# Fifteen blocks of an input projection moved ahead of attention and computed by fifteen products

## The chip, the core and the metric

The kernel runs on one core of one Trainium2 chip. The metric is the device time of one execution in microseconds (us), the median of several runs; lower is better. A core has one matrix engine (TensorE, PE in the profile, with its weight loads as PEld), three engines for elementwise work (VectorE is DVE, ScalarE is ACT, GpSimd is POOL) and queues that issue DMAs (SyncE is SP; here ACT issues some too). Each engine works through its own instructions in order, so an instruction that waits holds up all that stand behind it on that engine.

## What is computed

One layer of a streaming encoder for 1024 prompt frames and 32 sample frames, all in 32-bit floats. Both kinds of frames are treated together as T = 1056 columns. Cut to what matters here:

```
h = rmsnorm(x, g_mix) * (1 + sc1) + sh1
u = h @ w_in
qa, ka, va, qm, km, vm, om, ip, fp, ga, gm = split(u)
ya = band_attention(qa, ka, va)                      # 8 heads x 64
q_m, k_m = silu(causal_conv(concat(qm, km)))         # width 4
hm = mlstm(q_m, k_m, vm, ip, fp)                     # 4 heads x 128, a recurrence over blocks
ym = head_rmsnorm(hm) * sigmoid(om)
merged = sigmoid(ga) * (ya @ w_br_att) + sigmoid(gm) * (ym @ w_br_mlstm)
x = x + gt1 * (merged @ w_out)
x = x + gt2 * ((silu(h2 @ w_gate) * (h2 @ w_up)) @ w_down)
```

The gates `sc1`, `gt1` and so on are six vectors from `silu(c) @ w_ada + b_ada`.

## The kernel before

**Layout and blocks.** Features stand on the 128 partitions, the 1056 columns are cut in three thirds of 352 (`TILES`). A block of a projection is 128 output features. `unit` (L418) computes one third of one block: eight slices of 128 input features, and three matmuls for each slice (`PASSES`: high part times high, low times high, high times low, which is how the 32-bit product is kept accurate). So a plain block is 3 x 8 x 3 = 72 matmuls of 352 columns. The weights of a block are loaded (L404) and split in a high part by ACT (L394) and a low part by DVE or POOL (L395); `Weights` does that a fixed number of blocks ahead.

**Side work.** `unit` calls `side.tick()` after every second slice, so four times a third and twelve times a block. At a tick, generators started with `side.start(gen, steps, ticks, delay)` advance by `steps / ticks` steps. So the instructions of attention, of the recurrence and of the modulation are written between the matmuls of plain blocks, at a spacing that the table `segs` sets. All four compute engines keep exactly that order.

**The input projection.** The 40 blocks of q, k, v, convolution inputs, output gates `om` and merge gates `ga`, `gm` (and `vm` in two wide blocks, `vm_block`) are all computed plainly, in the order of `segs`: 3 blocks; then attention over pairs of heads 0, 1 and 2, beside 5, 5 and 7 blocks (three for the next q, k, v, the rest gates); attention 3 beside `vm_block(0)` and four convolution blocks; `mlstm(0)`, the recurrence of heads 0 and 1, beside `vm_block(1)` and four convolution blocks; and `mlstm(1)` followed by `branch_operands` beside twelve blocks (four `om`, eight gates). The modulation `ada_rest` (128 multiply-adds on DVE, L1139 and L1141, each two reading one DMA of 256 KB) runs beside all of this at 160 steps per 495 ticks.

**The recurrence.** `mlstm` goes through nine blocks of 128 columns. In the round for block i, a first step issues the scores and transposes of block i on PE (L1026, L1028) and the transposes of the result of block i-3 (L1096); a second step issues on DVE the scaling of result i-2 (L1090), the weighting of block i (L1044), and then the state update (L1070), the sum (L1073) and the denominators (L1077 to L1079) of block i-1, on PE the three products of block i-1 (L1056, L1059, L1061), on ACT its squares (L1082), and on POOL the two small operations that make the norm (L1084, L1085), which the scaling of the next round reads.

**The branch operands.** After `mlstm(1)`, for each of four blocks: sigmoid on ACT (L1183), a product on DVE (L1184), a split (L394 on ACT, L395 on DVE); then four splits of the attention result. The merge matmuls that follow read all of them.

**Fifteen products.** The feed-forward network already uses a scheme in which three blocks are computed together as a 3 x 2 by 2 x 3 product of sub-blocks with fifteen block products of 12 matmuls each (`Fifteen`, `fifteen_products`, `times` at L1726), 180 matmuls where plain blocks need 216. It needs sums of sub-blocks of the activations (`early_forms`, `late_forms`: sums at L1563 on DVE and POOL, high parts on ACT, low parts at L1576 on DVE) and sums of weight sub-blocks (L1361 on POOL).

## Time and profile before

| what | value |
| --- | --- |
| median of 3 runs | 1644.96 us (1642.6 to 1649.06) |
| the profiled execution | 1642.54 us |
| its span in the profile | 1640.6 us |
| PE busy | 1589.7 us (97%) |
| DVE busy | 1121.0 us (68%) |
| ACT busy | 780.8 us (48%) |
| POOL busy | 535.7 us (33%) |

The rows shown below come from five views: the page, the table of stretches (columns: from and to, length, then busy time of PE, PEld, DVE, ACT and POOL with their instruction counts, the granted clock of PE, the DMA share and GB/s), the groups by line (busy time and mean ns, then the idle time before them), the timeline (start, duration, engine, line, operation, tiles) and the chain that ended last. Since PE is busy nearly all the time, the question for any change is where PE starts to wait.

### The profile page before, as it was taken

To read this page: it belongs to the slowest core of one execution; us is meant where nothing else is said; L and a number is where in the kernel's file an instruction comes from. 1 tells how busy PE (TensorE), PEld (TensorE's weight loads), DVE (VectorE), ACT (ScalarE), POOL (GpSimd) and SP (SyncE) were. 2 spreads that over 40 slices of the span, in tenths; PEclk is the share of its full clock that TensorE was granted. 3 is DMA by queue.
4 is the path that set the end of the run, shared out by engine and by line. 5 is a ranking of instruction groups with operands and counts; after the bars stand their busy time and mean duration, and the time that the engine had idled before them with its cause. 6 is when DMAs were issued, how large, how long until landed. Compare 5 with 4: busy or idle time off the path is not lost.

```text
span 1640.6 us, 27517 instructions
## 1 busy us (share of the span) xinstructions
PE 1589.7 (97%) x10324; PEld 1566.7 (95%) x10324; DVE 1121.0 (68%) x2100; ACT 780.8 (48%) x1732; POOL 535.7 (33%) x540
## 2 busy tenths in 40 slices
PE   7989999999999999999999998999999999999997
PEld 6989999999999999999999988999999999999997
DVE  6756564546776744546655689889888986698754
ACT  3456454543455544444434645454545444444443
POOL 1234333333332311000012155566565742233101
PEclk9999999999999999999999999999999999999999
DMA  9732323232222332584453211313222236427453
GB/s 344 251 98 75 111 75 106 67 126 75 84 83 78 67 94 66 131 273 152 128 151 109 91 53 39 105 53 104 79 82 88 78 102 216 141 65 238 134 157 123
DMA packets 210326, 192.45 MB, mean 117 GB/s; under 512 B 10570, under 2 KB 180530, under 8 KB 209170
## 3 DMA queue, kind: packets, MB, share of 16 engines
q1 hardware_dynamic: 205970, 188.60, 36.8%
q10 hardware_dynamic: 4224, 2.10, 0.4%
q8 instruction: 81, 1.33, 0.4%
q14 instruction: 51, 0.42, 0.1%
HBM read 152.19 MB, written 41.63 MB: 118 GB/s over the span
## 4 chain that ended last, share of the span: by engine, by line
PE 79%; DVE 8%; ACT 3%; issue 2%; DMA 1%; POOL 1%; DVEq 0%; POOLq 0%; ACTq 0%
PE mm L428 35%; PE psb L1726 24%; PE psb L2082 5%; PE mm L825 3%; PE psb L1967 3%; PE psV L725 2%; PE psS L667 1%; DVE wsp L395 1%; PE psT L694 1%; DVE s L395 1%; DVE s L1576 1%; DVE s L1989 1%; DVE sl L1563 1%; DVE st L681 1%; PE psV L1059 1%
## 5 line engine op out<-in xcount | busy, mean ns | idle before, releaser
L428 PE MATMUL mm<-s,wsp 128*128 128x352 f32 x4104 | 690.4, 324 | 5.8 <-DVE t L1657 1.9
L428 PEld LDWEIGHTS mm<-s,wsp 128*128 128x128 f32 x4104 | 656.8, 188 | 9.0 <-DVE stg L518 2.3
L1726 PE MATMUL psb<-s,wsp 128*128 128x352 f32 x2544 | 422.0, 323 | 11.4 <-DVE s L1989 5.5
L1726 PEld LDWEIGHTS psb<-s,wsp 128*128 128x128 f32 x2544 | 410.9, 189 | 14.4 <-issue 6.1
L395 DVE TENSOR_TENSOR wsp<-wraw,wsp 128x512 fp32r<-128x512 f32 (+1 forms) x284 | 246.0, 884 | 136.0 <-ACT wsp L394 134.2
L394 ACT ACTIVATE wsp<-wraw 128x512 fp32r<-128x512 f32 x340 | 201.5, 617 | 147.6 <-PE psb L1726 84.5
L687 POOL TENSOR_SCALAR st<-st,mx 128x640 f32<-128x640 f32 (+5 forms) x72 | 57.0, 791 | 193.7 <-DVE mx L686 179.5
L1141 DVE SCALAR_TENSOR_TENSOR t<-wa,cmix,t 128x512 f32<-128x512 f32 x112 | 88.8, 797 | 8.9 <-DMA wa<-in_w_ada_dram 8.5
L395 POOL TENSOR_TENSOR wsp<-wraw,wsp 128x512 fp32r<-128x512 f32 x56 | 73.8, 1339 | 52.4 <-ACT wsp L394 52.0
L2082 PE MATMUL psb<-s,wsp 128*128 128x352 f32 x528 | 86.7, 324 | 0.0
L2082 PEld LDWEIGHTS psb<-s,wsp 128*128 128x128 f32 x528 | 84.7, 188 | 0.0
L681 DVE CUSTOM_DVE_ANT_0 st<-psS,bias 128x640 f32<-128x640 f32 (+5 forms) x72 | 44.5, 618 | 57.8 <-PE psS L667 44.9
L1726 PE MATMUL psb<-x,wsp 128*128 128x352 f32 x432 | 80.2, 325 | 2.3 <-DVE x L1576 2.3
L682 ACT ACTIVATE st<-st,mx 128x640 f32<-128x640 f32 (+5 forms) x72 | 47.9, 666 | 67.5 <-DVE mx L681 67.5
L1676 POOL TENSOR_TENSOR t<-t,sl 128x352 f32<-128x352 f32 x18 | 17.4, 969 | 185.3 <-ACT sl L1674 185.3
L1726 PEld LDWEIGHTS psb<-x,wsp 128*128 128x128 f32 x432 | 71.5, 189 | 2.8 <-DVE x L1576 2.8
L701 ACT ACTIVATE pT<-psT 128x640 fp32r<-128x640 f32 (+3 forms) x80 | 38.7, 494 | 72.1 <-PE psT L694 55.1
L1764 DVE TENSOR_TENSOR t<-t,psb 128x352 f32<-128x352 f32 x120 | 60.4, 512 | 5.2 <-PE psb L1726 4.8
L1361 POOL TENSOR_TENSOR wraw<-wraw 128x512 f32<-128x512 f32 x25 | 37.1, 1482 | 76.8 <-DVE wsp L395 75.8
L706 DVE TENSOR_TENSOR pT<-psT,pT 128x640 fp32r<-128x640 f32 (+3 forms) x80 | 44.0, 559 | 20.5 <-ACT pT L701 20.4
L1361 POOL TENSOR_TENSOR wraw<-wraw,raw 128x512 f32<-128x512 f32 x33 | 55.8, 1704 | 0.9
L825 PE MATMUL mm<-s,s 128*128 128x264 f32 (+3 forms) x432 | 54.9, 283 | 0.0
(340 smaller groups left out, 2334.2 us busy)
## 6 DMA issues: line engine op xcount, KB each, us to landing
wraw<-in_w_in_dram SPq DMA_DIRECT2D x40, 512.0 KB
wraw<-in_w_gate_up_dram SPq DMA_DIRECT2D x33, 512.0 KB
wa<-in_w_ada_dram SPq DMA_DIRECT2D x64, 256.0 KB
wraw<-in_w_down_dram SPq DMA_DIRECT2D x32, 512.0 KB
a_d<-t SPq DMA_DIRECT2D x22, 528.0 KB
g_d<-t SPq DMA_DIRECT2D x16, 528.0 KB
x<-xres SPq DMA_DIRECT2D x16, 528.0 KB
t<-g_d SPq DMA_DIRECT2D x16, 528.0 KB
```

The lines of the kernel that those rows point to most:

```text
L394: act.activation(dst[:, 0], src, AF.Copy)
L395: eng.tensor_tensor(dst[:, 1], src, f(dst[:, 0]), op=ALU.subtract)
L428: pe.matmul(pt[:, :hi - lo], wt[(w0 + k) // 4][:, a, (w0 + k) % 4], xt[k][:, b, lo:hi], start=(k == 0 and q == 0), stop=(k == n - 1 and q ...
L681: dve.tensor_tensor_reduce(so, sv, bi, -1.0, 3.0e38, ALU.add, ALU.min, mx[:n, 1:2])
L687: pool.tensor_scalar(st[:n, :w], st[:n, :w], mx[:n, 3:4], 1.0, op0=ALU.mult, op1=ALU.mult)
L825: pe.matmul(pt[:n, :wd], hs[k][:, a, i * P:i * P + n], whl[b][:, k, :wd], start=(k == 0 and q == 0), stop=(k == KD - 1 and q == 2))
L1141: dve.scalar_tensor_tensor(ac[:, c], wa, cmix[:, c, k:k + 1], ac[:, c], op0=ALU.mult, op1=ALU.add)
L1361: pool.tensor_tensor(a(dst), a(x), a(y), op=op)
L1726: pe.matmul(acc, wt[:, a, k], x[k][:, b], start=(start and not onto and k == 0 and q == 0), stop=(stop and k == 3 and q == 2), skip_group_ ...
L1764: dve.tensor_tensor(c, c, y, op=ALU.add if sign > 0 else ALU.subtract)
L1967: pe.matmul(acc, wt[k // 4][:, u, k % 4], piece_of[k, i][:, v], start=(k == 0 and q == 0), stop=(k == KP - 1 and q == 2))
L2082: pe.matmul(acc, wt[(k - k0) // 4][:, u, (k - k0) % 4], piece_of[k, 2][:, v], start=(k == 0 and q == 0), stop=(k == NF - 1 and q == 2))
```

## The change

- The 24 blocks that are only written to DRAM or can be (`kept`: four convolution blocks, four `om`, sixteen gates) leave the table. Six are computed plainly at the very start (`front`), beside the sums that the fifteen products need (`tk.early()`, then `tk.late_forms()`). Fifteen follow as five groups of fifteen products (`fifteen0`). Three stay in the table: one beside `mlstm(0)`, two beside `mlstm(1)`.
- The sums need h whole, so each block of h is completed on ACT (`whole_x`), in new tiles, and the thirds of h that late forms overwrite are stored in `h_d` and loaded and split again afterwards (`back`).
- After the products, the table runs: q, k, v of pair 0; attention 0, 1 and 2 beside only the three blocks of q, k, v each; attention 3 as before; `mlstm(0)` beside `vm_block(1)` and one block; `mlstm(1)` and `branch_operands` beside two blocks. The convolution inputs and `om` come back from DRAM (`conv_loaded`, `om_loads`).
- The modulation has a number of steps for each row of the table (36, 20, 20, 20, 56, 14, 0).
- The functions for the fifteen products move into a class `Tokens` that is used twice, otherwise unchanged.

```diff
+    def whole_x(j):
+        x = xns[j]
+        for c, a, b in col_segments(0, T):
+            act.activation(x[:, a:b], x[:, a:b], AF.Identity, bias=sh1[:, c, j:j + 1])
+        act.dma_start(h_d[j], x[:, thirds[1 + j // 4]])
...
+    kept = [(QM + b * P, u_d[b]) for b in (2, 6, 3, 7)] + [(OM + b * P, o_d[b]) for b in range(4)] + gates
+    NFRONT, NROWS = 6, 15
+    front = [raw_block(*x, *((slots,) if i == 2 else ())) for i, x in enumerate(kept[:NFRONT - 1])]
+    front.append(raw_block(*kept[NFRONT - 1], None, (1, 2, 0), lambda: start_late()))
+    rows0 = kept[NFRONT:NFRONT + NROWS]
+    rest = [raw_block(*x) for x in kept[NFRONT + NROWS:]]
...
     segs = [
-        (nothing, b_qkv(0), None, 0),
-        (nothing, mix(b_qkv(1), b_gates(0, 2)), lambda: attention(0), ATT_STEPS),
-        (nothing, mix(b_qkv(2), b_gates(2, 4)), lambda: attention(1), ATT_STEPS),
-        (nothing, b_qkv(3) + b_gates(4, 8), lambda: attention(2), ATT_STEPS),
+        (nothing, b_qkv(0), None, 0, 36),
+        (nothing, b_qkv(1), lambda: attention(0), ATT_STEPS, 20),
+        (nothing, b_qkv(2), lambda: attention(1), ATT_STEPS, 20),
+        (nothing, b_qkv(3), lambda: attention(2), ATT_STEPS, 20),
...
-        (open_mls, [vm_block(1), conv_block(2), conv_block(6), conv_block(3), conv_block(7)],
-         lambda: mlstm(0), ML_STEPS),
-        (nothing, [om_block(b) for b in range(4)] + b_gates(8, 16),
-         lambda: chain(mlstm(1), conv_rows(), branch_operands()), ML_STEPS + BR_STEPS + 3),
+         lambda: attention(3), ATT_STEPS, 56),
+        (open_mls, [vm_block(1)] + rest[:1], lambda: mlstm(0), ML_STEPS, 14),
+        (om_loads, rest[1:],
+         lambda: chain(mlstm(1), conv_rows(), branch_operands()), ML_STEPS + BR_STEPS + 3, 0),
...
+    fifteen0 = [Fifteen([w_in[:, c0:c0 + P] for c0, _ in rows0[i:i + 3]]) for i in range(0, NROWS, 3)]
...
+    tk = Tokens(hs, xq)
+    first_units([run.w for run in front[:2]])
...
+    tk.job = side.start(tk.early(), 9, 10)
+    for run in front:
+        run()
...
+    for i, x in enumerate(fifteen0):
+        rows, done = [tmpt(), hk_row(), tmpt()], [0, 0, 0]
...
+        fifteen_products(tk, x, rows, third_done)
...
+    for j in range(KD):
+        sp.dma_start(back[j], h_d[j])
...
+    for run in segs[0][1][:2]:
+        first[id(run.w), 0] = unit(run.w, 0, hs, *TILES[0])
+    for j in range(KD):
+        split_to(hs[j][:, :, thirds[1 + j // 4]], back[j])
```

Three places show how the order on the engines moves. The first is PE in the middle of `mlstm(1)`, one round of the recurrence: the scores (L1026, now L1057) and transposes of one block, up to the state product (L1056, now L1087) of the block before it, with a plain block's matmuls (L428, now L448) between. Before:

```order
L1026 MATMUL psS_6915<-s_6067 128x128
L1028 MATMUL psS_6915<-ident,s_6067 128x128
L1096 MATMUL mm_6927<-ident,num_6780 128x128 x2
L428 MATMUL mm_6942<-s_479,wsp_6747 128x352 x3
L428 MATMUL mm_6942<-s_505,wsp_6747 128x352 x3
L428 MATMUL mm_6942<-s_531,wsp_6747 128x352 x3
L428 MATMUL mm_6942<-s_556,wsp_6747 128x352 x3
L428 MATMUL mm_6942<-s_582,wsp_6748 128x352 x3
L428 MATMUL mm_6942<-s_607,wsp_6748 128x352 x3
L1056 MATMUL psT_6965<-C_6871,s_5630 128x129
```

And the same engine at the same place in the changed kernel:

```order
L1092 MATMUL psT_8009<-s_6861,W_7942 128x129 x2
L1057 MATMUL psS_8035<-s_6957 128x128
L1059 MATMUL psS_8035<-ident,s_6957 128x128
L1057 MATMUL psS_8035<-s_7562 128x128
L1059 MATMUL psS_8035<-ident,s_7562 128x128
L1127 MATMUL mm_8047<-ident,num_7965 128x128 x2
L448 MATMUL mm_7928<-s_583,wsp_7513 128x352 x3
L448 MATMUL mm_7928<-s_611,wsp_7513 128x352 x3
L1087 MATMUL psT_8061<-C_8020,s_6957 128x129
```

Eighteen matmuls stood there, six do now, and ahead of the scores, where eighteen more stood, none do.

The second place is DVE between the last sums of the products and the first scores of attention 0 in the changed kernel. L525 makes the low part of k from PSUM, L1170 and L1172 are the modulation, L671 makes the low part of q that the first scores read; `back` and `s` ahead of these rows are the restored thirds of h.

```order
L411 TENSOR_TENSOR s_674<-back_2687,s_674 128x352
L525 TENSOR_TENSOR s_2770<-mm_2704,s_2770 64x352 x2
L1170 TENSOR_SCALAR t_2783<-wa_2784,cmix 128x512 x2
L1172 SCALAR_TENSOR_TENSOR t_2783<-wa_2800,cmix,t_2783 128x512 x2
L1172 SCALAR_TENSOR_TENSOR t_2783<-wa_2810,cmix,t_2783 128x512
L525 TENSOR_TENSOR s_2770<-mm_2776,s_2770 64x352 x2
L1172 SCALAR_TENSOR_TENSOR t_2783<-wa_2810,cmix,t_2783 128x512
L1172 SCALAR_TENSOR_TENSOR t_2783<-wa_2832,cmix,t_2783 128x512 x2
```

Before, the same engine has no modulation at all there (its first row, L1139, stood behind L645, the low part of q):

```order
L502 TENSOR_TENSOR s_688<-mm_477,s_688 64x352 x2
L502 TENSOR_TENSOR s_688<-mm_478,s_688 64x352 x2
L518 COPY stg_757<-mm_755 32x128
L546 TENSOR_TENSOR s_778<-mm_779,s_778 128x8x64
L546 TENSOR_TENSOR s_778<-mm_792,s_778 128x8x64
```

In the changed kernel 32 of the modulation's instructions, four of L1170 and 28 of L1172, stand in this stretch ahead of L671.

The third place is PE at the end of `mlstm(1)` in the changed kernel: the last state product (L1087), the last two transposes of the result (L1127), the transpose for the convolution rows (L1251), and what is left of the plain blocks.

```order
L1087 MATMUL psT_8213<-Cs_7762,s_7562 32x129
L1090 MATMUL psV_8214<-vms,kw_8148 128x129 x2
L1092 MATMUL psT_8213<-vms,W_8144 32x129 x2
L1127 MATMUL mm_8237<-ident,num_8167 128x128 x2
L448 MATMUL mm_8195<-s_527,wsp_7699 128x352 x3
L448 MATMUL mm_8195<-s_555,wsp_7699 128x352 x3
L1127 MATMUL mm_8250<-ident,num_8221 128x32 x2
L448 MATMUL mm_8195<-s_583,wsp_7700 128x352 x3
L448 MATMUL mm_8195<-s_611,wsp_7700 128x352 x3
L1251 MATMUL mm_8265<-ident,ncv 48x128
```

Behind the last of these rows 54 matmuls of the plain blocks are left in the changed kernel, and then the merge begins; before, 264 stood behind the convolution rows' transpose.

522 lines of the change are left out of this document (292 added, 230 removed), and 8 rows, old and new, of the table PARTS.

## The prediction

> **What bounds the kernel now.** First the page's head and the table of stretches: where does PE wait?
>
> ```profile
> span 1640.6 us, 27517 instructions
> 92.00:184.00 92.00, 87.81 (x583) 83.96 (x582) 56.67 (x134) 47.25 (x109) 33.05 (x43) 1.00 0.30 89
> 184.00:271.00 87.00, 85.91 (x575) 83.08 (x574) 50.24 (x127) 44.95 (x106) 32.14 (x40) 1.00 0.29 88
> 271.00:369.00 98.00, 96.38 (x647) 94.54 (x646) 50.79 (x128) 48.55 (x113) 37.40 (x41) 1.00 0.31 94
> 369.00:474.00 105.00, 101.84 (x729) 99.06 (x728) 72.78 (x193) 49.48 (x114) 37.19 (x59) 1.00 0.24 71
> 474.00:590.00 116.00, 116.00 (x837) 114.34 (x836) 78.10 (x168) 61.93 (x162) 38.39 (x57) 1.00 0.34 89
> 590.00:712.00 122.00, 122.00 (x817) 120.48 (x817) 63.85 (x152) 56.71 (x152) 10.98 (x22) 1.00 0.38 102
> 925.00:1020.00 95.00, 85.23 (x522) 83.56 (x521) 82.67 (x145) 51.65 (x124) 44.79 (x36) 0.98 0.13 40
> 1020.00:1430.00 410.00, 407.27 (x2532) 407.00 (x2530) 338.58 (x500) 201.94 (x404) 217.02 (x139) 1.00 0.33 105
> ```
>
> Attention (92 to 474 us) and both recurrences (474 to 712) run at PE's pace: idle is 10.1 us in the first and none in the second. Matmuls of plain blocks cover every chain of the side work. Only where the sums for the fifteen products are made (925 to 1020) does PE wait 9.8 us, with DVE busy 82.67 of 95. So time falls by what PE is spared, as long as what is left on PE still covers the side work. The chain that ended last gives the paces:
>
> ```profile
> 709.78 147.50 PE mm L428 x918
> 1018.85 354.32 PE psb L1726 x2197
> ```
>
> A matmul of 352 columns takes 147.50 / 918 = 0.161 us in plain blocks and 354.32 / 2197 = 0.161 us in products.
>
> **What the change takes off PE.** Fifteen blocks are 15 x 72 = 1080 matmuls, five groups are 5 x 180 = 900: 180 x 0.161 = **-29**. Can the side work of products follow? A group takes PE 29 us.
>
> ```profile
> L395 DVE TENSOR_TENSOR wsp<-wraw,wsp 128x512 fp32r<-128x512 f32 (+1 forms) x284 | 246.0, 884 | 136.0 <-ACT wsp L394 134.2
> L1764 DVE TENSOR_TENSOR t<-t,psb 128x352 f32<-128x352 f32 x120 | 60.4, 512 | 5.2 <-PE psb L1726 4.8
> ```
>
> DVE has 15 splits of 0.884 us and 15 sums of 0.512 us, 21 us of 29, without the feed-forward products of L1793: it follows, as it did from 1020 to 1430. All else that PE did stays. The rest of the sum is waiting.
>
> **Token forms beside six blocks.** The same sums cost 9.8 us of waiting in the feed-forward network, some of it from the second norm. Beside the last four front blocks (288 matmuls, 46 us) DVE has them again, without that norm. I take **+7**, between 2 and 11; ACT's `whole_x` is hidden under the eighteen matmuls (2.9 us) of each step of `first_units`; uncovered, it would add some 1 us a step.
>
> **Reloading h.** Eight loads of 176 KB wait for the last product; two thirds (48 matmuls, 7.7 us) cover them. **+2**, between 0 and 6.
>
> **q, k, v of pair 0.** The window of DVE groups from 75 to 474 us gives:
>
> ```profile
> L1141 DVE SCALAR_TENSOR_TENSOR t<-wa,cmix,t 128x512 f32<-128x512 f32 x65 | 53.3, 822 | 0.4
> L645 DVE TENSOR_TENSOR s<-t,s 64x1056 fp32r<-64x1056 f32 x8 | 10.7, 1340 | 0.1
> L502 DVE TENSOR_TENSOR s<-mm,s 64x352 fp32r<-64x352 f32 x20 | 10.5, 523 | 6.6 <-ACT kf L500 6.4
> ```
>
> 28 multiply-adds at 0.822 (23 us), four first products and six L502 (5), L645 twice (2.7) and some seven more for v and the caches: 38 us ahead of the first scores, while PE has the 168 matmuls left after the reload, 27 us, and a few transposes. DVE comes 8 to 10 us late, and the first scores wait for L645 behind it: **+8**, between 2 and 16 (the modulation's loads pass two buffers only).
>
> **Attention.** Attention 0 to 2 hold PE 270.1 us in the three rows above, of which 17 plain blocks are 17 x 72 x 0.161 = 197. With nine blocks left, 73 + 104 = 177 us, 59 for each. DVE needs 157.7 / 3 = 53 of it, with about the same share of the modulation. That is 90% in order, so some waits must appear; attention 3 gets 29 more steps of modulation (23 us), 96 of 102. **+8** in all, between 0 and 24, nearer the low end because DVE stays below PE.
>
> **The recurrence** is the term that decides. One round of `mlstm(1)` in the timeline:
>
> ```profile
> 605.04 0.19 POOL L1084 TENSOR_SCALAR dn<-dn 128x2 f32<-128x2 f32 x1 [20.37 <-ACT sq L1082]
> ...
> 608.40 0.61 PE L1056 MATMUL psT<-C,s 128*128 128x129 f32 x4
> ...
> 609.57 0.60 DVE L1090 TENSOR_SCALAR num<-num,dn 128x128 f32<-128x128 f32 x2
> ...
> 609.65 3.14 PE L428 MATMUL mm<-s,wsp 128*128 128x352 f32 x18
> ...
> 610.08 0.42 DVE L1044 SCALAR_TENSOR_TENSOR W<-psS,W 128x256 f32<-128x256 f32 x1
> 610.41 0.60 DVE L1070 SCALAR_TENSOR_TENSOR C<-C,wc,psV 128x129 f32<-128x129 f32 x2
> 610.93 0.42 DVE L1073 TENSOR_TENSOR num<-num,psT 128x258 f32<-128x258 f32 x1
> ...
> 611.77 0.17 DVE L1079 RECIPROCAL dn<-dn 128x2 f32<-128x2 f32 x1
> ...
> 612.03 0.40 ACT L1082 ACTIVATE sq<-num,dn 128x128 f32<-128x128 f32 x1 [1.47 <-DVE dn L1079]
> ...
> 612.63 0.38 PE L1026 MATMUL psS<-s 128*128 128x128 f32 x2
> ...
> 613.14 0.69 POOL L1084 TENSOR_SCALAR dn<-dn 128x2 f32<-128x2 f32 x1 [7.11 <-ACT sq L1082]
> ...
> 613.43 3.13 PE L428 MATMUL mm<-s,wsp 128*128 128x352 f32 x18
> ...
> 613.91 0.70 POOL L1085 TENSOR_TENSOR dn<-dn,mhalf 128x2 f32<-128x2 f32 x1
> 614.64 0.60 DVE L1090 TENSOR_SCALAR num<-num,dn 128x128 f32<-128x128 f32 x2 [0.87 <-POOL dn L1085]
> ```
>
> This is a ring: DVE scales, weighs, updates the state, sums and inverts; ACT squares; POOL makes the norm; and DVE's next scaling waits for POOL, with the next state update queued behind it. From 609.57 to 614.64 no step waits for PE: 5.07 us, 4.6 where L1084 takes 0.19, as in the round before (first row). I take 4.85. PE's own share of a round is 608.40 to 609.65 and 612.63 to 613.43, 2.05 us. Before, two runs of 18 matmuls made a round about 7.8 us, longer than the ring. By the order, the eight rounds of `mlstm(1)` now hold 36 plain matmuls in all: 16.4 + 5.8 = 22 us on PE against a ring of 38.8, so 17 us of waiting, and 2 more at its two ends: **+19**, between 14 and 26. In `mlstm(0)` the eight rounds hold 66 narrower and 24 plain matmuls.
>
> ```profile
> L825 PE MATMUL mm<-s,s 128*128 128x264 f32 (+3 forms) x432 | 54.9, 283 | 0.0
> ```
>
> At 54.9 / 432 = 0.127 us, 8.4 + 3.9 + 16.4 = 28.7 against 38.8: **+10**, between 5 and 18; 14 steps of modulation and the late convolutions fit mostly where DVE waits for POOL.
>
> **The branch operands.** Here is one of four, with 264 matmuls behind it before and 54 now:
>
> ```profile
> 684.46 1.28 ACT L1183 ACT_TABLE_LOAD   x1
> ...
> 698.88 1.08 ACT L1183 ACTIVATE s<-s 128x1056 f32<-128x1056 f32 x1
> 699.99 1.56 DVE L1184 TENSOR_TENSOR s<-s,s 128x1056 f32<-128x1056 f32 x1 [0.93 <-ACT s L1183]
> 701.59 1.08 ACT L394 ACTIVATE s<-s 128x1056 fp32r<-128x1056 f32 x1 [1.63 <-DVE s L1184]
> 702.71 1.26 DVE L395 TENSOR_TENSOR s<-s,s 128x1056 fp32r<-128x1056 f32 x1 [1.15 <-ACT s L394]
> ```
>
> Sigmoid, product and high part take 3.6 us a block without waits; with the table, four blocks and four splits of 1.26, 1.3 + 14.4 + 5 = 21 us, against 54 x 0.161 = 8.7 and the first merge half, 1.9: **+10**, between 7 and 14.
>
> **The clock.** The granted clock after the waits of the feed-forward sums:
>
> ```profile
> 985.00:1000.00 15.00, 12.97 (x82) 12.62 (x80) 13.83 (x25) 8.34 (x21) 7.89 (x6) 1.00 0.18 56
> 1000.00:1020.00 20.00, 15.87 (x91) 15.12 (x91) 18.24 (x24) 9.59 (x23) 15.33 (x10) 0.88 0.04 12
> ```
>
> It stayed at 1.00 with PE busy 12.97 of 15 and fell to 0.88 at 15.87 of 20. I put **+2** on the long waits, between 0 and 15. [...]
>
> **The sum.** -29 + 7 + 2 + 8 + 8 + 19 + 10 + 10 + 2 = +37. The profiled execution took 1642.5 us (1.9 more than its span), 2.4 under the median of the runs; 1679.5 on its scale, **1682** on that of the median: 2.2% slower.
>
> **Rivals.**
> *The ring is hidden.* If the scaling of a round does not hold the next state update, a round of the recurrence costs what PE has in it, 2.8 to 3.6 us, and the 19 and 10 go, with the clock's 2: 1651, within 0.5% of 1645, so not slower. The point is a ring of about 3.2 us, and each 0.1 us above it costs 1.6 us over sixteen rounds. Against it speaks this row of the waits between 486 and 680 us (waiter, releaser, us in total, times, longest):
>
> ```profile
> DVE num L1090 <- POOL dn L1085: 7.9, 9, 1.0
> ```
>
> In half of the eighteen rounds the ring already holds DVE up. 0.15.
> *Every queue has slack.* If the weight tiles split ahead and PSUM also hide the lateness of DVE up to attention 3 (25 us), and the ring is short: about 1626, faster. DVE at 90% speaks against it. 0.12.
> *DVE bounds attention.* Waits at 8 us a pair instead of 2: four times 6 more, 1706. The share of 96 of 102 in attention 3 speaks for it. 0.12.
> *The clock halves in the rounds.* PE's 2.8 us become 5.6, past the ring of 4.85, over sixteen rounds: +12, 1694. The 0.88 above speaks for it, the 1.00 beside 12.97 of 15 against it. 0.06. [...]
> *The products spare nothing*, because DVE paces them: 29 more, 1711. The 21 of 29 us speak against it. 0.03.
>
> **How the numbers follow.** The forecast has 0.52. Half a per cent is about what a measurement of this kernel can tell from no change. Slower: 0.52 + 0.12 + 0.06 + 0.03 = 0.73; same 0.15; faster 0.12. The range leaves out the faster rival and about 0.08 above: 1640 to 1712. The forecast's own range is 1660 to 1705.
>
> **What would show it.** Right: in the changed profile, rounds of the recurrence 4.6 to 5.1 us apart with PE waiting on DVE or ACT in each; PE waiting some 10 us ahead of the first merge, on the branch operands; the first scores waiting on DVE's low part of q; products at 0.161 us. Wrong: no PE waits of over 1 us in the recurrence, or rounds of 3 to 3.6 us; or a wait that no term names, such as loads of h or of the convolution inputs that SP issues late.

## The result, and the profile after

The changed kernel takes 1786.39 us (median of 4 runs, 1778.56 to 1790.54) against 1643.78 us before: a ratio of 1.0856, 95% interval 1.0810 to 1.0903. It is slower, as forecast, but by 143 us where the prediction had 37, far beyond its range. The profiled execution took 1790.54 us, 1.7 more than its span.

The page's row of the granted clock after the change, in 40 slices of the span of 1788.8 us (before, all of them were 9):

```profile
PEclk9899999898989999988799999999999999999999
```

The table of stretches after the change, cut at the stages: the end of `first_units`, the first product, the last product, the first scores of attention, the first matmul of `vm_block(0)`, the first scores of `mlstm(0)`, those of `mlstm(1)`, the merge (taken where ACT starts its first sigmoid; PE has done the first 12 matmuls of the merge by then). Each row gives the stretch, its length, then busy time and count of PE, PEld, DVE, ACT and POOL, the granted clock, DMA share and GB/s.

```profile
75.00:127.10 52.10, 48.48 (x291) 47.90 (x289) 42.89 (x57) 23.41 (x54) 28.75 (x26) 0.97 0.32 106
127.10:282.40 155.30, 148.26 (x900) 146.68 (x900) 118.86 (x174) 67.56 (x132) 83.51 (x54) 0.98 0.30 98
282.40:339.10 56.70, 45.23 (x262) 43.08 (x261) 32.36 (x53) 19.54 (x42) 16.88 (x17) 0.94 0.59 185
339.10:587.00 247.90, 203.37 (x1250) 188.48 (x1249) 160.62 (x385) 121.11 (x289) 84.95 (x108) 0.91 0.22 69
587.00:712.80 125.80, 118.59 (x828) 114.40 (x829) 95.68 (x230) 53.46 (x125) 47.52 (x71) 0.96 0.31 94
712.80:786.60 73.80, 62.16 (x413) 57.83 (x412) 41.02 (x124) 44.10 (x124) 19.03 (x39) 0.88 0.30 63
786.60:876.20 89.60, 53.38 (x306) 48.73 (x306) 46.09 (x121) 49.26 (x128) 7.97 (x18) 0.78 0.45 136
876.20:1788.80 912.60, 883.40 (x5487) 878.97 (x5486) 685.25 (x1107) 421.17 (x883) 325.77 (x248) 0.99 0.36 113
```

The same stages before (q of pair 0, attention 0 to 2, attention 3, both recurrences, the rest):

```profile
73.70:93.80 20.10, 19.61 (x127) 19.10 (x127) 7.06 (x14) 13.52 (x29) 10.15 (x14) 1.00 0.47 142
93.80:374.40 280.60, 271.52 (x1809) 262.71 (x1807) 156.98 (x384) 140.55 (x329) 106.45 (x130) 1.00 0.30 92
374.40:489.00 114.60, 113.62 (x837) 111.13 (x838) 84.86 (x209) 54.77 (x124) 39.80 (x58) 1.00 0.27 78
489.00:730.50 241.50, 241.50 (x1641) 238.32 (x1640) 135.20 (x310) 118.97 (x312) 42.25 (x71) 1.00 0.40 112
730.50:1640.60 910.10, 882.48 (x5500) 877.36 (x5498) 683.06 (x1107) 423.13 (x885) 328.35 (x248) 0.99 0.36 115
```

The prediction's terms can now be laid against stages. A stage's forecast is its length before, plus or minus the 72-matmul blocks that come or go (11.6 us each), plus the term:

| stage | forecast, us | measured | off |
|---|---|---|---|
| up to the end of `first_units` | 73.7 | 75.0 | +1 |
| four front blocks and 15 products: 46.4 + 144.9 + 7 | 198.3 | 207.4 | +9 |
| h back, q, k, v of pair 0: 20.1 + 23.2 + 2 + 8 | 53.3 | 56.7 | +3 |
| attention 0 to 2: 280.6 - 92.7 + 6 | 193.9 | 247.9 | **+54** |
| attention 3: 114.6 + 2 | 116.6 | 125.8 | +9 |
| recurrences up to the merge: 241.5 - 13 x 11.6 + 39 | 129.7 | 163.4 | **+34** |
| merge to end (clock + 2) | 912.1 | 912.6 | 0 |

So 88 of the 111 us missing from the forecast's span of 1677.6 lie in two stages. In both, the granted clock fell as well (0.91, and 0.88 and 0.78). In attention 0 to 2 the same matmuls take PE 203.4 us instead of 271.5 - 92.7 = 178.8, so 24.6 us are slower matmuls; PE idles 44.5 us instead of 9.1.

Where does PE wait in attention? This is the timeline at the start of attention 1 (idle time and its releaser in brackets):

```profile
420.64 3.00 POOL L607 TENSOR_SCALAR s<-s 64x352 fp32r<-64x352 f32 x2 [2.30 <-ACT s L605]
...
423.72 2.50 POOL L411 TENSOR_TENSOR wsp<-wraw,wsp 128x512 fp32r<-128x512 f32 x2
426.31 0.61 POOL L1176 TENSOR_SCALAR wa<-t 64x512 f32<-64x512 f32 x1
...
427.65 0.14 POOL L660 MEMSET bias<- 64x64 f32 x1
427.83 0.29 DVE L707 CUSTOM_DVE_ANT_0 st<-psS,bias 128x128 f32<-128x128 f32 x1 [4.54 <-POOL bias L660]
...
428.19 0.79 PE L693 MATMUL psS<-s,s 128*128 128x256 f32 x2 [3.43 <-DVE mx L707]
```

The change left q as the last block before the next pair's attention; before, a gate block stood behind it. Now q's copies, a weight split and the swap of the modulation stand on POOL ahead of the bias mask, DVE's softmax waits for the mask, and PE waits 3.4 us for the one PSUM tile of scores. The first 14 us of attention 1, first after the change, then before it:

```profile
421.80:436.00 14.20, 10.50 (x53) 9.72 (x53) 5.25 (x16) 3.42 (x10) 7.50 (x11) 0.76 0.45 132
```

```profile
183.00:197.00 14.00, 14.00 (x94) 13.78 (x93) 9.36 (x27) 7.66 (x20) 5.40 (x6) 1.00 0.14 39
```

53 matmuls instead of 94, at a clock of 0.76. The starts of pairs 0 and 2 look alike (30 matmuls in 14.2 us at a clock of 0.64, 41 in 13.4 us at 0.79). The rest of each pair waits less, in many small pieces, mostly for L732, L707 and L759 on DVE.

### The profile page after: what moved, and what is told of

Its sections match the earlier page's. It is cut to its first block, busy times and chain, and to the rows that moved or that the text cites. A ratio compares the mean times of both kernels' runs of the same rounds, so it can differ in the third digit from the quotient of the medians.

```text
span 1788.8 us, 27759 instructions
## 1 busy us (share of the span) xinstructions
PE 1625.3 (91%) x10144; PEld 1586.1 (89%) x10144; DVE 1273.3 (71%) x2317; ACT 837.4 (47%) x1838; POOL 627.0 (35%) x603
## 4 chain that ended last, share of the span: by engine, by line
PE 60%; DVE 15%; DMA 8%; ACT 7%; issue 4%; POOL 3%; SPq 1%; ACTq 0%; DVEq 0%; POOLq 0%
PE psb L1605 29%; PE mm L448 18%; PE psb L2197 5%; PE psb L2082 3%; DVE t L1172 2%; DVE st L707 2%; DVE wsp L411 2%; DMA rb_d<-in_rel_bias_dram 1%; ACT st L708 1%; DMA wa<-in_w_ada_dram 1%; DMA out_dram<-C 1%; DMA wraw<-in_w_in_dram 1%; PE psT L720 1%; DVE s L1012 1%; PE psV L751 1%
## 5 line engine op out<-in xcount | busy, mean ns | idle before, releaser
L448 PE MATMUL mm<-s,wsp 128*128 128x352 f32 x3024 | 536.5, 334 | 25.8 <-ACT t L620 13.4
L1605 PE MATMUL psb<-s,wsp 128*128 128x352 f32 x3264 | 545.5, 325 | 15.4 <-DVE wsp L411 6.5
L1605 PEld LDWEIGHTS psb<-s,wsp 128*128 128x128 f32 x3264 | 530.9, 190 | 18.8 <-DVE wsp L411 8.0
L448 PEld LDWEIGHTS mm<-s,wsp 128*128 128x128 f32 x3024 | 505.3, 196 | 32.0 <-ACT t L620 13.8
L411 DVE TENSOR_TENSOR wsp<-wraw,wsp 128x512 fp32r<-128x512 f32 (+1 forms) x319 | 288.6, 919 | 117.9 <-ACT wsp L410 115.0
L410 ACT ACTIVATE wsp<-wraw 128x512 fp32r<-128x512 f32 (+1 forms) x359 | 214.9, 618 | 191.7 <-PE psb L1605 119.2
L1605 PE MATMUL psb<-x,wsp 128*128 128x352 f32 x612 | 113.6, 324 | 7.7 <-ACT x L1496 4.8
L713 POOL TENSOR_SCALAR st<-st,mx 128x640 f32<-128x640 f32 (+5 forms) x72 | 53.8, 747 | 190.2 <-DVE mx L712 163.3
L1605 PEld LDWEIGHTS psb<-x,wsp 128*128 128x128 f32 x612 | 101.0, 188 | 8.7 <-ACT x L1496 5.1
L1172 DVE SCALAR_TENSOR_TENSOR t<-wa,cmix,t 128x512 f32<-128x512 f32 x112 | 91.0, 837 | 10.1 <-DMA wa<-in_w_ada_dram 9.6
L1383 POOL TENSOR_TENSOR wraw<-wraw 128x512 f32<-128x512 f32 x36 | 52.8, 1467 | 118.5 <-DVE wsp L411 117.2
L2197 PE MATMUL psb<-s,wsp 128*128 128x352 f32 x528 | 86.7, 324 | 0.0
L2197 PEld LDWEIGHTS psb<-s,wsp 128*128 128x128 f32 x528 | 84.7, 188 | 0.0
L707 DVE CUSTOM_DVE_ANT_0 st<-psS,bias 128x640 f32<-128x640 f32 (+5 forms) x72 | 44.3, 616 | 37.6 <-PE psS L693 16.5
L411 DVE TENSOR_TENSOR wsp<-raw,wsp 128x512 fp32r<-128x512 f32 x60 | 60.2, 1004 | 8.6 <-ACT wsp L410 8.1
L1641 ACT ACTIVATE t<-psb 128x352 f32<-128x352 f32 x102 | 43.8, 464 | 44.1 <-DVE t L1643 23.3
```

The source lines that it names most:

```text
L410: act.activation(dst[:, 0], src, AF.Copy)
L411: eng.tensor_tensor(dst[:, 1], src, f(dst[:, 0]), op=ALU.subtract)
L448: pe.matmul(pt[:, :hi - lo], wt[(w0 + k) // 4][:, a, (w0 + k) % 4], xt[k][:, b, lo:hi], start=(i == 0 and q == 0), stop=(i == n - 1 and q ...
L707: dve.tensor_tensor_reduce(so, sv, bi, -1.0, 3.0e38, ALU.add, ALU.min, mx[:n, 1:2])
L713: pool.tensor_scalar(st[:n, :w], st[:n, :w], mx[:n, 3:4], 1.0, op0=ALU.mult, op1=ALU.mult)
L1172: dve.scalar_tensor_tensor(ac[:, c], wa, cmix[:, c, k:k + 1], ac[:, c], op0=ALU.mult, op1=ALU.add)
```

## The experiments

All kernels are the change with the edit shown. Times are medians of two runs (of four for `mended`), each beside the kernel before on the same chip; the change's own runs spread over 12 us, so a few microseconds in a total tell nothing, and verdicts are read from the stages. How far a stage can be trusted shows where an edit leaves it alone: attention 0 to 2 is 247.9 to 249.5 us in five such kernels, the recurrences are 163.3 to 163.6 in four, but 168.2 in ada_later. The stages in us, from the profiles:

| run | time | ratio (95%) | products | q, k, v | attention 0-2 | attention 3 | recurrences |
|---|---|---|---|---|---|---|---|
| the change | 1786.4 | 1.086 (1.081-1.090) | 155.3 | 56.7 | 247.9 | 125.8 | 163.4 |
| nine_attention | 1753.5 | 1.066 (1.063-1.069) | 66.9 | 59.7 | 294.3 | 121.3 | 163.6 |
| nine_recurrence | 1741.5 | 1.059 (1.052-1.065) | 66.9 | 56.7 | 247.9 | 130.1 | 206.6 |
| three_after_q | 1752.6 | 1.063 (1.059-1.067) | 126.7 | 62.8 | 233.0 | 125.2 | 163.6 |
| one_group | 1722.9 | 1.045 (1.042-1.048) | 39.6 | 58.7 | 282.6 | 123.9 | 182.9 |
| splits_on_dve | 1789.4 | 1.088 (1.081-1.094) | 155.3 | 56.5 | 244.4 | 123.7 | 169.7 |
| half_modulation | 1767.5 | 1.074 (1.070-1.078) | 155.1 | 51.1 | 235.6 | 118.5 | 161.2 |
| no_low_part | 1780.6 | 1.082 (1.079-1.084) | 155.2 | 56.4 | 240.2 | 126.4 | 163.4 |
| ada_later | 1783.2 | 1.083 (1.080-1.087) | 155.9 | 43.1 | 252.4 | 122.2 | 168.2 |
| filler | 1889.8 | 1.148 (1.145-1.151) | 153.6 | 56.9 | 319.1 | 148.1 | 166.8 |
| wide_filler | 1810.5 | 1.098 (1.095-1.101) | 155.4 | 59.5 | 264.4 | 124.4 | 163.3 |
| scaled_last | 1785.4 | 1.084 (1.081-1.088) | 153.6 | 56.8 | 248.6 | 124.3 | 163.3 |
| state_on_act | 1794.8 | 1.091 (1.088-1.094) | 155.0 | 56.4 | 247.9 | 125.3 | 167.2 |
| ya_on_act | 1794.2 | 1.090 (1.087-1.093) | 153.5 | 56.4 | 248.1 | 125.0 | 168.3 |
| no_ya_load | 1780.9 | 1.080 (1.077-1.083) | 155.2 | 56.4 | 249.5 | 124.3 | 155.1 |
| mended | 1736.7 | 1.054 (1.052-1.056) | 97.3 | 56.3 | 249.8 | 122.7 | 171.9 |

### Blocks put back beside attention, and beside the recurrences

```diff
-    NFRONT, NROWS = 6, 15
+    NFRONT, NROWS = 6, 6
...
-        (nothing, b_qkv(1), lambda: attention(0), ATT_STEPS, 20),
+        (nothing, mix(b_qkv(1), rest[:2]), lambda: attention(0), ATT_STEPS, 20),
...
-        (nothing, b_qkv(3), lambda: attention(2), ATT_STEPS, 20),
+        (nothing, b_qkv(3) + rest[4:9], lambda: attention(2), ATT_STEPS, 20),
```

> Two groups of products instead of five; the nine blocks freed run as plain blocks beside attention 0 to 2 again, the recurrences keep the change's three. The products take about 3 x 31 = 93 us less. Theory A (attention lost its cover; plain blocks run in the waits and keep the granted clock up): attention 0 to 2 goes from 248 us to what it took before with 17 blocks, 281, and some 12 for the ninth block more, so about 45 us come back; 1786 - 93 + 45 = 1738 in all, and the granted clock there is 1.00. Theory B (attention is slow for another reason, such as the modulation or the reloaded h): nine blocks cost 9 x 11.6 = 104 us there, 1797.

For nine_recurrence, also with six rows, the nine go to the other stage:

```diff
-        (open_mls, [vm_block(1)] + rest[:1], lambda: mlstm(0), ML_STEPS, 14),
-        (om_loads, rest[1:],
+        (open_mls, [vm_block(1)] + rest[:5], lambda: mlstm(0), ML_STEPS, 14),
+        (om_loads, rest[5:],
```

> Two groups of products instead of five; the nine blocks freed run as plain blocks beside the two recurrences (five more beside the first, seven in all beside the second), attention stays as thin as in the change. Theory A (the recurrences and branch operands wait too, 164 us with PE busy 116 and the clock at 0.72 to 0.88): of 104 us of blocks only some 40 add to the stage; 1786 - 93 + 40 = 1733. Theory B (the recurrences' waits are at places that plain blocks don't reach, behind loads that SP issues late): 104 us are added, 1797. Attention 0 to 2 stays at about 248 us in both.

Attention 0 to 2 of nine_attention, and both recurrences of nine_recurrence:

```profile
254.30:548.60 294.30, 285.16 (x1882) 277.16 (x1880) 155.37 (x384) 142.97 (x334) 103.52 (x127) 0.99 0.30 89
```

```profile
629.40:836.00 206.60, 199.81 (x1340) 195.12 (x1339) 95.39 (x255) 109.97 (x290) 35.48 (x59) 0.98 0.48 125
```

Theory A held both times. Nine blocks, 104 us of matmuls, add 294.3 - 247.9 = 46.4 us beside attention and 206.6 - 163.4 = 43.2 beside the recurrences: 5.2 and 4.8 us for a block. A row of the products costs 155.3 / 15 = 10.4. The totals fell less than forecast, by some 15 and 8 us; 5 of these are the nine rows, which took 88 us out of the products and not 93.

### Three blocks right behind q

```diff
-    NFRONT, NROWS = 6, 15
+    NFRONT, NROWS = 6, 12
...
-        (nothing, b_qkv(0), None, 0, 36),
+        (nothing, b_qkv(0) + rest[:1], None, 0, 36),
-        (nothing, b_qkv(1), lambda: attention(0), ATT_STEPS, 20),
+        (nothing, b_qkv(1) + rest[1:2], lambda: attention(0), ATT_STEPS, 20),
...
```

> Four groups of products instead of five; the three blocks freed stand right behind q of pairs 0, 1 and 2, where attention of that pair starts. The products take 31 us less. Theory A (the starts of the pairs cost most: q's copies, its low part, the weight split and the bias mask in line, while PE has nothing else): the blocks fill these waits, 7 us at pair 0 and 3.4 at each of the others with the slow clock behind them, so they add 12 us or less: about 1764. Theory B (the waits are spread over all steps): a block costs what each of the nine cost on average, 5 us, or more: 15 to 20 us, about 1772. If the waits were no use to them, 35 us: 1790.

```profile
252.80:315.60 62.80, 56.67 (x339) 54.90 (x339) 38.06 (x58) 23.86 (x48) 19.95 (x20) 0.95 0.59 185
315.60:548.60 233.00, 210.78 (x1390) 198.05 (x1388) 152.42 (x380) 123.25 (x296) 83.42 (x111) 0.99 0.28 82
```

The two stretches together take 295.8 us instead of 304.6: three blocks more, 9 us less. The clock is 0.99 instead of 0.91. So a block at this place costs less than nothing, which is theory A, and more than it said. But not only the starts gain: from its first scores to those of the next, attention 2, whose start is covered and which has no block of its own, takes 76.8 us instead of 81.9 (to the end of the stage); attention 1, with a block in it, 75.3 instead of 82.7; attention 0, also with a block in it, 80.9 instead of 83.3. So with its start covered a pair took 75 to 81 us here, and whether PE had 59 us of work for it or 71 did not decide it.

### Which engine holds the start: weight splits on DVE

```diff
     W.ahead = 2
-    on_pool[0] = True
```

> The low parts of the weight tiles beside attention are taken by DVE instead of POOL. At the start of attention 1 and 2 the first mask of the bias stands on POOL behind two copies of q (L607, 3.0 us) and two weight splits (L411, 2.5 us); DVE's softmax waits for it 4.5 us and PE 3.4. Theory A (POOL's queue is what the pair's start waits for): 2.5 us less at each of three starts and a shorter stretch of the slow clock behind it, 8 to 20 us in all, about 1772. Rival (DVE bounds attention): some 40 splits of 0.55 us come on top of DVE, up to 22 us more, about 1800.

Attention 0 to 2 gains 3.5 us, the total nothing. The start of attention 1 shows why:

```profile
423.82 2.07 DVE L411 TENSOR_TENSOR wsp<-wraw,wsp 128x512 fp32r<-128x512 f32 x2 [2.84 <-ACT wsp L410]
...
425.82 2.53 DVE L671 TENSOR_TENSOR s<-t,s 64x1056 fp32r<-64x1056 f32 x2
427.11 0.33 PE L693 MATMUL psS<-s,s 128*128 128x128 f32 x1 [2.37 <-DVE s L671]
```

The mask is ready at 425.6, but now q's low part stands behind the split on DVE. Neither forecast holds: POOL's queue is not the cause by itself, as the work between q's last matmul and the first scores has to be done somewhere, and the splits did not make attention longer on DVE either.

### Is it DVE, or the chain of a step?

half_modulation leaves out half of the multiply-adds on DVE, no_low_part the low part of attention's weights:

```diff
-                    else:
+                    elif k < 4:
                         dve.scalar_tensor_tensor(ac[:, c], wa, cmix[:, c, k:k + 1], ac[:, c],
```

> Leaves out the multiply-adds of the modulation for the rows k = 4 to 7 of each chunk, half of them (64 x 0.82 = 52 us of DVE in all); loads and steps stay. Theory A (DVE's work bounds attention and the stretch ahead of it): about 25 us less in attention 0 to 2, 15 ahead of it, 20 in attention 3: 1730. Theory B (in attention the step's chain from scores to transposes and the queue of POOL set the pace, and DVE has idle time): under 10 us in attention 0 to 2, some 10 ahead of the first scores; 1765 to 1780.

```diff
-            for m, a, b in cuts:
-                dve.tensor_tensor(pv[:m, 1, a:b], pT[:m, a:b], f(pv[:m, 0, a:b]), op=ALU.subtract)
+            pass
...
```

> Leaves out the low part of attention's weights (L732 on DVE, 0.57 us in each step); the values multiply the high part twice, so PE has the same work. Attention 0 to 2 takes 248 us in the change. Theory A (a step's own chain sets the pace there: transposes, scores, softmax on DVE, the low part behind it on DVE, and the next transposes into the one PSUM tile that the low part frees): 0.4 to 0.6 us less in each of 63 steps, 25 to 36 us in attention 0 to 2, and less in attention 3, where plain blocks cover: 1750 to 1760. Theory B (only the starts of the pairs and the modulation on DVE count): under 12 us less there, 1775 to 1786.

Attention 0 to 2 in each:

```profile
333.80:569.40 235.60, 199.85 (x1251) 184.97 (x1249) 140.03 (x358) 121.00 (x288) 82.75 (x108) 0.93 0.24 72
```

```profile
338.20:578.40 240.20, 200.30 (x1250) 186.28 (x1249) 131.52 (x326) 120.08 (x288) 85.24 (x108) 0.92 0.24 71
```

Taking 20.6 us (160.62 - 140.03) off DVE gains 12.3; taking 29.1 us off it in the middle of each step gains 7.7. In half_modulation both theories fall short, as DVE counts for more than B allowed and for less than A said. In no_low_part the number is that of theory B (under 12), and theory A, that a step's own chain sets the pace, was wrong by a factor of three or more. The rows of waits show where the gain went, first the change, then no_low_part:

```profile
DVE mx L712 <- ACT st L708: 20.4, 43, 0.7
```

```profile
DVE mx L712 <- ACT st L708: 48.4, 54, 1.5
```

(The second window reaches 7 us into attention 3; up to 578.4 the row is the same.) Without its low part, DVE waits more for ACT's exponentials. That a whole step's way through the engines sets the pace fits these rows but is not shown by them. What the trace shows besides is that no engine alone holds the stage: in the chain that ended last between 339 and 587 us of the change, PE's rows have some 36%, DVE's at least 23% and ACT's at least 11%.

### Modulation away from q, k, v of pair 0

```diff
-        (nothing, b_qkv(0), None, 0, 36),
+        (nothing, b_qkv(0), None, 0, 0),
-        (nothing, b_qkv(1), lambda: attention(0), ATT_STEPS, 20),
+        (nothing, b_qkv(1), lambda: attention(0), ATT_STEPS, 32),
...
```

> No step of the modulation beside q, k, v of pair 0; 32 instead of 20 beside each of attention 0 to 2. From the last product to the first scores the change takes 56.7 us, with 216 matmuls (35 us) for PE. Theory A (the modulation's loads and multiply-adds hold DVE up there): about 43 us, 13 less, and attention 0 to 2 takes up the 36 steps with under 8 us, as DVE has 20 to 30% idle: 1775 in all. Rival 1 (the reloaded h and the caches set that stretch): 55 us, no gain. Rival 2 (DVE bounds attention): 13 us less there and 20 to 30 more in attention, 1800.

```profile
281.30:324.40 43.10, 40.83 (x253) 39.29 (x253) 10.45 (x21) 19.57 (x42) 13.50 (x15) 1.00 0.50 158
```

Theory A, nearly to the microsecond: 13.6 us less here, 4.5 more in attention. (The recurrences came out 5 us longer without an edit there; the total gained 3.)

### Is it the clock?

Two kernels keep PE busier with matmuls that nobody reads. The first puts them where PE waits:

```diff
+    def fill(pt, c0, n, times):
+        for _ in range(times):
+            pe.matmul(pt[:, c0:c0 + n], hs[0][:, 0, :P], hs[0][:, 0, :n], start=True, stop=True)
...
                 pvs[i - 2] = (pv, w)
+                fill(pT, 672, NT, 4)
...
```

> The change, with matmuls whose result nobody reads added behind the transposes of each step of attention (4 of 352 columns, into unused columns of the same PSUM tile) and in each round of the recurrences (6 of 256 and 6 of 254 columns). At the full clock they are 72 x 4 x 0.161 = 46 us and 18 x 1.4 = 25 us of PE. In attention 0 to 2 of the change PE is busy 203.5 us of 248, where the same matmuls at the full clock would take 177. Theory A (the slow clock costs time by itself: waits drop it, and slow matmuls lengthen the chains): with the waits filled the clock stays near 1.00, and attention 0 to 2 takes under 240 us though PE has 35 us more to do. Theory B (the chains of attention's steps set the pace, and the slow matmuls only fill what would be waits): 245 to 260 us, and the whole time 1780 to 1800. Theory C (PE is the bound there): the 71 us are added, 1850.

In attention it failed as an experiment: the stage grew by 71 us, as the filler itself waited, for ACT's reading of other columns of the tile that it was put into:

```profile
PE psT L666 <- ACT pT L731: 50.3, 54, 2.5
```

In the first recurrence it worked:

```profile
805.90:880.20 74.30, 68.18 (x520) 65.33 (x519) 39.61 (x122) 42.23 (x123) 17.84 (x34) 0.98 0.27 51
```

The clock is 0.98 instead of 0.88, there are 107 matmuls more, and the stage takes 74.3 us instead of 73.8. So the full clock brought nothing that the added matmuls didn't take again. The likeliest reading is that the slow matmuls only fill what would be waits, but the run can't part that from a gain which the filler used up.

The second adds its matmuls to plain blocks, in columns that those don't use. With them k, q and v come out wrong, so that only the time counts:

```diff
             if i % 2 == 1:
+                for _ in range(wide[0]):
+                    pe.matmul(pt[:, NT:], wt[0][:, 0, 0], xt[0][:, 0, :512 - NT], start=True, stop=True,
+                              skip_group_check=True)
                 side.tick()
...
```

> The change, with six matmuls of 160 columns more at each of the 108 points of the plain blocks beside attention 0 to 2 where a step of attention can begin, into the columns of the block's own PSUM tile that it doesn't use, so that nothing waits for them: 648 x 0.161 x 160 / 352 = 47 us of PE at the full clock. Nobody reads them. Attention 0 to 2 takes 248 us in the change. Theory A (the slow clock costs time by itself): PE waits less, the clock stays near 1.00 and the stage takes under 243 us in spite of more work. Theory B (latencies of the attention steps set 248 us and the slow clock only fills waits): 246 to 258 us. Theory C (added plain work counts as in the run with nine blocks put back beside attention, 46 us for 104): 264 to 274 us.

Its timeline, where L456 is the filler, and the row of the stage:

```profile
560.05 0.79 PE L456 MATMUL mm<-s,wsp 128*128 128x160 f32 x6
560.68 1.16 PE L450 MATMUL mm<-s,wsp 128*128 128x352 f32 x6
```

```profile
342.70:607.10 264.40, 253.32 (x1882) 247.68 (x1880) 159.41 (x384) 119.15 (x286) 83.64 (x107) 0.99 0.22 66
```

Six of them take 0.63 us (from 560.05 to 560.68), so the filler is 68 us, not 47. The stage is 16.5 us longer: 51 us went into waits and slow stretches. Theory A is not tested by this: at the full clock PE has 178.8 + 68 = 247 us to do, already more than the 243 that A allowed. The number falls into C's range, though C's filler was smaller. How much of the 24.6 us of slow matmuls would be left as waits at the full clock, these runs can't say.

### The recurrences: the ring, and its ends

scaled_last issues the scaling, which waits for POOL's norm, behind the next state update:

```diff
-            if 0 <= i - 2 < NB:
-                num, dn, n, t0 = b.pop(i - 2)
-                scaled(num, dn, n)
-                c[i - 2] = (num, n, t0)
             if i < NB:
                 weigh(a[i][0], a[i][1], a[i][3])
...
+            if 0 <= i - 2 < NB:
+                num, dn, n, t0 = b.pop(i - 2)
+                scaled(num, dn, n)
+                c[i - 2] = (num, n, t0)
```

> The change with one move in the recurrence: the scaling of a round's result (L1121, which waits for POOL's norm) is issued on DVE behind the state update and the sums of the next round instead of ahead of them. Theory A (the ring that the prediction named: no round can be shorter than DVE, ACT's squares and POOL's norm one after the other, with the next state update behind the scaling): rounds fall from 4.7 us to 3.2 to 3.8, over some 17 rounds 15 to 25 us less, about 1766. Rival (ACT's eviction of the sums, the weight splits or PE at half clock set the round): 4.4 us and more, under 6 us less.

Theory A falls, and the rival's number holds. By the first scores of six rounds, a round takes (829.3 - 800.5) / 6 = 4.80 us in the change and (830.0 - 802.5) / 6 = 4.58 here. Where the wait went, from 796 to 832 us, shows in one row of the change and two of scaled_last:

```profile
DVE num L1121 <- POOL dn L1116: 8.5, 5, 1.7
```

```profile
DVE W L1075 <- ACT kw L1069: 12.3, 8, 3.7
...
PE mm L1127 <- DVE num L1121: 4.2, 5, 1.3
```

DVE no longer waits for POOL, but now for ACT, which issues squares, exponential and weighted k in this order. And PE's transposes of the result (L1127), ahead of the products in PE's order, now wait for the scaling that was moved back, which they never did in this stretch of the change. So the edit opened one ring and made another wait; how short a round is with the first ring open and nothing put in its place stays open.

The start of the second recurrence has a wait that no term of the prediction names. The change's chain that ended last, and the end of it in PE's timeline:

```profile
765.38 9.65 DMA out_dram<-C
775.10 10.52 DMA t<-u_d
```

```profile
793.19 0.80 PE L1057 MATMUL psS<-s 128*128 128x128 f32 x2 [6.10 <-ACT s L1017]
```

The convolution inputs (`u_d`) are loaded behind the stores of the first recurrence's state, and ACT and DVE still have the convolution to do when they land. (The expectation of state_on_act below counts 10.9 us more of waiting there; in PE's timeline these are 66 matmuls of a plain block, so no wait.)

At the merge the change has this, from the chain that ended last and from PE's timeline:

```profile
845.84 8.50 DMA out_dram<-C
856.59 7.74 DMA t<-ya_d
...
866.81 6.61 DMA t<-ya_d
```

```profile
874.93 5.35 PE L448 MATMUL mm<-s,wsp 128*128 128x352 f32 x17 [13.39 <-ACT t L620]
```

PE has by then done the 12 matmuls of the merge's first product that read the gated result (it waited 3.2 us for their operands); the 13.39 us are ahead of the 12 that read attention's output. ACT's last eviction of a plain block stands behind the splits of attention's output, these wait for loads, and the loads stand on SP behind reloads of x that wait for the stores of C (SP waited 7.7 us for one at L1772). Three edits: stores of C by ACT; loads of `ya_d` by ACT, two of them early; no such loads at all.

```diff
-                sp.dma_start(oc[0, 0, h0 + hh], C[:, hh, :P])
+                act.dma_start(oc[0, 0, h0 + hh], C[:, hh, :P])
...
```

> The stores of the recurrence's state go to ACT's queue instead of SP's. Theory A (loads of the convolution inputs and of the attention output stand behind the stores on SP): the two long waits, 10.9 + 6.1 us ahead of the second recurrence and 13.4 us ahead of the merge, shrink by half or more: 12 to 25 us less, about 1768. Rival (the loads wait for their buffers or for bandwidth): under 5 us less, 1782 to 1788.

```diff
+        def ya_load():
+            raws.append(tmpt())
+            act.dma_start(raws[-1], ya_d[len(raws) - 1])
+        ya_load()
+        ya_load()
...
-            sp.dma_start(raw, ya_d[b])
```

> The loads of attention's output for the merge are issued by ACT, the first two ahead of the branch operands, instead of by SP, where they stand behind reloads of x that wait for the state's stores. From the last scores of the second recurrence to the merge the change takes 46.5 us. Theory A (that queue order is what PE waits for ahead of the merge, 13.4 us): 8 to 13 us less, about 1775. Rival (the branch operands' own sigmoid, products and splits, which cover the loads): under 4 us less.

```diff
-            raw = tmpt()
-            sp.dma_start(raw, ya_d[b])
             y = slot([P, 2, T], F32R)
-            split_to(y, raw)
+            split_to(y, om[b // 2][:, b % 2])
```

> Leaves out the four loads of attention's output ahead of the merge; its operand is made of the gate's product instead (four splits as before, with a wrong operand). From the last scores of the second recurrence to the merge the change takes 46.5 us, with PE waiting 13.4 us in one piece for an eviction that ACT does behind these splits. Theory A (the loads, 7 to 10 us from issue to landing through two free buffers, hold ACT): 8 to 12 us less, about 1776. Theory B (ACT and DVE need that long for eight operands, 3.6 us for each of four and 2.4 for the others): under 4 us less.

From the last scores to the merge: 46.5 us in the change, 52.9 with the stores on ACT, 48.5 with the loads on ACT, 35.6 without loads. So the loads hold the merge (theory A of no_ya_load), but not for the queue that was suspected, and theory A of the two others falls. With the stores on ACT the 6.10 us at the second recurrence shrink to 3.9, but the end grows by more. With the loads on ACT two of them are issued at 863.84 and 867.27, behind ACT's other work, and land 7 us later.

```profile
863.84 0.33 ACTq L1212 DMA_DIRECT2D t<-ya_d  x1
...
871.06 1.09 ACT L410 ACTIVATE s<-t 128x1056 fp32r<-128x1056 f32 x1 [4.34 <-DMA t<-ya_d]
```

### Fewer groups, and three mends together

one_group keeps one group of products; of twelve blocks freed, eight run beside attention, as many as before, and four beside the recurrences:

```diff
-    NFRONT, NROWS = 6, 15
+    NFRONT, NROWS = 6, 3
...
+        (nothing, b_qkv(3) + rest[4:8], lambda: attention(2), ATT_STEPS, 20),
...
+        (open_mls, [vm_block(1)] + rest[8:11], lambda: mlstm(0), ML_STEPS, 14),
```

> One group of products instead of five; of the twelve blocks freed eight run beside attention 0 to 2 (17 there, as before the change), two more beside the first recurrence and two more beside the second. The products take 4 x 31 = 124 us less. If attention 0 to 2 returns to the pace of before (281 us, 33 more) and the four others cost 4.8 us each as the nine did: 33 + 19 back, 1786 - 124 + 52 = 1714. If covered time is gone after the first few blocks: 33 + 46, 1741. What then stays above 1645 is what the change costs apart from thin stages: the token forms, the reload, q, k, v of pair 0 with the modulation beside them, and the recurrences with twelve blocks less than before.

1722.9 us, near the 1714 of the first forecast: the products fell by 116 us instead of 124, and the four blocks beside the recurrences cost 4.9 us each. Attention 0 to 2 takes 282.6 us, against 280.6 before the change: with its blocks back, nothing of the 54 us is left. The other 79 us over the kernel before are, on the spans: recurrences 182.9 against 241.5 - 9 x 11.6 = 137.1, so 46; q, k, v with the reload and the modulation 58.7 against 43.3, 15; the front and the one group 167.2 against 154.9, 12; attention 3 9; the rest -3.

mended has three groups, three blocks behind q, three more beside the recurrences, the modulation moved as in ada_later and the scaling as in scaled_last:

```diff
-    NFRONT, NROWS = 6, 15
+    NFRONT, NROWS = 6, 9
...
+        (nothing, b_qkv(0) + rest[:1], None, 0, 0),
+        (nothing, b_qkv(1) + rest[1:2], lambda: attention(0), ATT_STEPS, 32),
+        (nothing, b_qkv(2) + rest[2:3], lambda: attention(1), ATT_STEPS, 32),
+        (nothing, b_qkv(3), lambda: attention(2), ATT_STEPS, 32),
...
```

> Three groups of products instead of five; of the six blocks freed three stand behind q of pairs 0, 1 and 2, one more runs beside the first recurrence and two more beside the second; no modulation beside q, k, v of pair 0 (32 steps instead of 20 beside each of attention 0 to 2), and the scaling of a round behind the next state update. By the parts measured: three blocks behind q with one group less -38, modulation -10, the second group -29 with three blocks at 4.8 us each +14, the round 0 to -25: 1703 to 1726 if the parts add. If they share their gain, as the modulation moves into the waits that the blocks fill, 1730.

1736.7 us: the parts don't add. Attention 0 to 2 takes 249.8 us instead of the 233.0 of three_after_q, where the 36 steps of modulation moved there are the only difference of edit in the stage; DVE has 177.5 us of work in it instead of 152.4. In ada_later, where the waits were still empty, the same move cost 4.5 us, and here, where blocks fill them, 17. No kernel here comes near the one before.

## Why the prediction was wrong in size

**The sign and the first terms** were right. Fifteen rows took 155.3 us as products against 15 x 11.6 = 174 as plain blocks, 18.7 of the 29 us saved; with the front the term was 9 us off. The rival that products spare nothing is out.

**q, k, v of pair 0** (+2, +8): 3 us off, by the cause named. The first scores waited 7.07 us for L671, and without the modulation the stage is 13.6 us shorter.

**Attention** (+8, "nearer the low end because DVE stays below PE"): this is the step that failed. It came to 60 us in attention 0 to 2 (247.9 against 280.6 - 92.7) and 11 in attention 3. The step compared the sums of two engines, 59 us on PE and 53 on DVE for a pair, took the larger and put a little waiting on it. But a pair left with only its own blocks takes 82 to 83 us: eight blocks, 92.7 us of matmuls, left this stage, and only 32.7 us of time went with them. Shown by nine_attention and one_group: blocks put back cost 4 to 5 us each, so they stand in waits. What makes the waits is shown in parts only: the starts of the pairs (the start was charged once, at pair 0, and the block behind q that had covered the others went too; three blocks there made two stages 9 us shorter), the modulation on DVE (12.3 us for half of it), the low part on DVE (7.7 us). That what is left comes of each step's way through PE, DVE, ACT, DVE, POOL, PE, ACT and DVE, with each queue in order, is argued from the rows of waits; no run shows it. The rival that DVE bounds attention had the place right and part of the cause: DVE is busy 160.6 of 247.9 us, so it is no bound, but its work counts, most where the waits are filled (mended).

**The recurrences** (+19, +10, +10): 163.4 - (241.5 - 150.8) = 72.7 where 39 stood. The period was right: 4.80 us in six rounds of the second, forecast 4.85, range 4.6 to 5.1. The mechanism was so in part: the wait of DVE for POOL is there, but without it DVE waits for ACT instead (scaled_last), so "the ring is hidden" could not have come true by this move. What failed is the rest of the sum. It counted sixteen rounds, 77.6 us; they took 86.7, as five of them took 5.4 to 9.3 us, the longest the one with the 6.10 us for the convolution inputs. And the ends outside the rounds took 76.7 instead of the 52.1 that the forecast left. Of these 25 us no_ya_load shows 11; the other 14 were not taken apart by a run and stay open. PE's waiting for the branch operands themselves (+10) is 3.2 us; the 13.39 behind it is the eviction held up by loads. Late loads the prediction had only as a sign of being wrong, and that sign came true twice.

**The clock** (+2): it fell far more than forecast, to 0.91, 0.88 and 0.78 in three stages. The 2 was the author's estimate, and no run shows it as a term of its own. What the runs showed in its place: 24.6 us of slower matmuls in attention 0 to 2, and a first recurrence that took 74.3 us at 0.98, with 107 matmuls more, and 73.8 at 0.88 (filler). The rival that it halves in the rounds was right that it can (0.50 from 806 to 808 us) and wrong about the price: six rounds with a mean clock of 0.88 (800.5 to 829.3 us) took 4.80 us each, where that rival had 5.6. In attention its price stays open. The forecast put its 2 on long waits; the rows in the last section show the clock at 0.50 behind waits of 2 us too.

**The range** stopped at 1712, as no rival let a displaced block cost more at its new place than it had cost at the old one: 10.4 us as a row of products, against the 32.7 us that went with eight blocks of attention 0 to 2 (4.1 each) and the 78.1 that went with thirteen of the recurrences (6.0 each).

## What to carry to other kernels

A block of work that fills another stage's waits costs only what it adds to that stage, here 5 us of its 11.6; what a move gains is that, minus what the block costs at its new place, whatever its length. Before taking cover away from a stage, find out how long it is without cover: the largest sum of busy time is only a lower bound (59 us against 82 here). Following one step through all its engines may give it; that was not tried here. Running the stage with fewer blocks gives it surely. Where a chain's start is exposed, one block put right there can be worth more than its own length.
